# Scale maxima through memory, two jobs' score maxima beside the convolution, and gating and residual adds on GpSimd, in a two-layer hybrid backbone

## The chip, the cores and the metric

One core of one Trainium2 chip runs the whole kernel. TensorE multiplies, VectorE, ScalarE and GpSimd do elementwise work and reductions, and nearly every DMA is issued from SyncE's queue (SP). The metric is the device time of one execution in microseconds.

## The reference

A stream of 2048 latent tokens and 256 context tokens of width 1024 goes through two layers, in float32. What matters of it:

```
for layer in range(2):
    shift, scale, gate = split(silu(c) @ w_mod + b_mod)
    p = split_cols((rms_norm(h, norm_g) * (1 + scale) + shift) @ w_in)   # 1024 -> 3584 columns
    y_conv = p.cb * short_conv(p.cc * p.cv, conv_w) * silu(p.cz)         # width 3 over positions
    att    = softmax(q k^T / 8) v          # 4 heads of 64, 2 key heads; rms_norm and rotary on q, k
    hg     = rms_norm(forward + backward HGRN2 scan)                     # chunks of 64
    y_four = real part of the 2-D DFT over positions and channels
    y = concat(y_conv, att * silu(az), hg * silu(hz), y_four * silu(fz)) @ w_out
    h = h + gate * y                       # the context stream likewise, except in layer 1
out = rms_norm(h, final_g)
```

## The kernel before

Every matrix of float32 numbers is split into two float16 halves (high and low) after scaling by a power of two, and a product is three products of halves: high by high, low by high, high by low. The power of two comes from the largest absolute value of the matrix.

**A scale maximum.** `wsplit` (L385) takes a block of 256 columns of w_in: `absmax` (L153) gives the largest value in each of 128 partitions (VectorE), L391 joins the two halves, `rowmax` (L137) transposes the column of 128 into one row on TensorE and reduces it on VectorE (L142), `spread` (L145) multiplies that number by a row of ones on TensorE, so that every partition has it, and copies it out (L150). `pow2` makes the scale; ScalarE casts the high half (L406), VectorE makes the low half (L407). The same is done for the attention's values (`att_values`, L900), for w_out (`out_wmax`, L1557), and in `out_open` (L1587), where six bounds are transposed at once and give the scale of the output projection's input.

**A layer's stages.** `layer` (L1376) runs, one after another: the HGRN2 projections and forward scan; the reverse scan with gates and Fourier projections (`hg_reverse`); the Fourier transform; the attention projection (`att_block`, with gates, the maxima of w_out and four blocks of weights); then the convolution's projections (`conv_block`), the attention's four jobs of 512 queries, and the output projection (`out_tile`, 18 tiles of 128 tokens, 16 in layer 1).

A job has two parts. `att_max` (L931) computes scores of 128 queries by 512 keys on TensorE (L941) into two banks tagged "tr" and reduces each to its row maximum on VectorE (L942), 80 of them; the maxima are transposed and sent by DMA into two rows of Q2 (L960). `att_core` (L966) computes scores again with those rows in the product (L1016, L1017), takes the exponential on ScalarE (L1019), casts its high half on ScalarE (L1025) or VectorE (L1023), makes the low half on VectorE (L1026) and multiplies by the values (L983, L984), 72 steps for a job.

`weave` calls generators in turns, spread over a common course; an entry is (number of steps, generator, from, to). So the stages before the change are:

```
weave(values, maxima of job 0, a third of the convolution)
weave(core(jobs[0]), mx(jobs[1]), the rest of the convolution)
weave(core(jobs[1]), mx(jobs[2]), out_open, out tiles up to T[0] = 5)
weave(core(jobs[2]), mx(jobs[3]), out tiles up to T[1] = 8)
weave(core(jobs[3]), out tiles up to T[2] = 12)
```

and the remaining tiles go, in layer 0, beside the first weights and norms of layer 1 (`start`, L1396). The calls' order is a wish: the framework orders each engine's instructions by it and by its own estimate of when operands are there, so an engine may take a later call first. Within one engine, SP's queue too, instructions then start strictly in that order.

An output tile: `out_load` reads heads' outputs and gates, `out_prep` (L1259) multiplies them (L1266), splits the product and transposes both halves by DMA (L1271, L1272); 48 products of 512 columns follow (L1306), and VectorE multiplies by the gate vector (L1310) and adds the residual (L1311), half a tile each.

## Time and profile before

| | us |
|---|---|
| median of 3 runs | 2727.41 (2725.93 to 2731.69) |
| the profiled execution | 2724.91 |
| its span, first to last instruction | 2721.5 |
| TensorE busy | 2576.0 |
| VectorE busy | 2147.0 |
| ScalarE busy | 1495.4 |
| GpSimd busy | 105.0 |

The rows further below name engines PE (TensorE), DVE (VectorE), ACT (ScalarE), POOL (GpSimd) and SP. Matmuls overlap and their ends are modelled, so the spacing of their starts says more than their durations. An arrow points from what an instruction reads to what it writes, or from an idle time to what ended it.

### The profile page before, as it was taken

The numbers are of one execution on the slowest core, as the hardware profiler recorded it, in microseconds if no ns is written. First come the engines' busy times: TensorE is split into PE (matmuls) and PEld (weight loads), VectorE is DVE, ScalarE is ACT, GpSimd is POOL, SyncE is SP. The second block draws the span as 40 slices with busy tenths as digits, with TensorE's granted clock in tenths as the row PEclk, the third lists the DMA queues.
The fourth block names the chain that finished last, engine by engine and source line by source line (L and its number), as shares of the span: only waits on it lengthen the run. The fifth ranks groups of instructions, "written<-read, shape, count | busy, mean of one in ns | idle before, by whom it ended". The sixth has DMA issues, their size and how long they took to land. (4 is left out here: it accounts for less than half of the span.)

```text
span 2721.5 us, 67137 instructions
## 1 busy us (share of the span) xinstructions
PE 2576.0 (95%) x28046; PEld 1915.2 (70%) x28046; DVE 2147.0 (79%) x4707; ACT 1495.4 (55%) x2789; POOL 105.0 (4%) x108
## 2 busy tenths in 40 slices
PE   6999999999999999999999999999988999999998
PEld 3788877888777875555547888878877787455553
DVE  5888765777698669899877888768678876999885
ACT  2877532322226647798837666423221565879782
POOL 0000001011000000000000000010110000000000
PEclk8999999999999999999999999999999999999999
DMA  6111158353411015224281111344333100423425
GB/s 218 56 49 49 37 187 266 116 152 103 113 38 56 16 45 170 77 72 130 55 247 56 48 49 33 101 131 148 110 92 95 40 25 22 145 79 77 115 52 156
DMA packets 268680, 260.32 MB, mean 96 GB/s; under 512 B 95316, under 2 KB 237656, under 8 KB 268376
## 3 DMA queue, kind: packets, MB, share of 16 engines
q1 hardware_dynamic: 268376, 256.04, 31.5%
q8 instruction: 219, 3.59, 0.5%
q14 instruction: 85, 0.70, 0.1%
HBM read 168.59 MB, written 67.13 MB: 87 GB/s over the span
## 5 line engine op out<-in xcount | busy, mean ns | idle before, releaser
L431 PE MATMUL psmm<-xh,wh 128*128 128x256 f16 x2208 | 608.1, 275 | 7.8 <-DVE xh L357 6.1
L432 PE MATMUL psmm<-xl,wh 128*128 128x256 f16 x2208 | 606.7, 275 | 1.5 <-DVE xl L358 1.5
L433 PE MATMUL psmm<-xh,wl 128*128 128x256 f16 x2208 | 606.5, 275 | 0.7 <-DVE wl L407 0.7
L1019 ACT ACTIVATE aP<-pssc,pshift,ascale 128x512 f32<-128x512 f32 (+1 forms) x584 | 444.6, 778 | 221.6 <-PE pssc L1017 193.2
L445 PE MATMUL psmm<-wh,xh 128*128 128x256 f16 x1664 | 459.1, 276 | 5.6 <-ACT av L818 4.2
L1026 DVE TENSOR_TENSOR apl<-aP,aph 128x512 f16<-128x512 f32 (+1 forms) x584 | 390.2, 681 | 86.8 <-ACT aph L1025 82.6
L446 PE MATMUL psmm<-wl,xh 128*128 128x256 f16 x1664 | 458.4, 275 | 0.0
L447 PE MATMUL psmm<-wh,xl 128*128 128x256 f16 x1664 | 458.2, 275 | 0.0
L942 DVE TENSOR_REDUCE amx<-pstr 128x1 f32<-128x512 f32 (+1 forms) x648 | 391.5, 627 | 46.5 <-PE pstr L941 45.1
L1025 ACT CAST aph<-aP 128x512 f16<-128x512 f32 (+1 forms) x508 | 305.5, 619 | 9.6
L983 PE MATMUL pspv<-V,aph 128*128 128x129 f16 x2320 | 298.7, 221 | 1.4 <-DVE aph L1023 1.2
L984 PE MATMUL pspv<-V,apl 128*128 128x65 f16 x2320 | 269.6, 193 | 4.9 <-DVE apl L1026 3.6
L984 PEld LDWEIGHTS <-apl 128*128 128x128 f16 x2320 | 206.6, 98 | 84.4 <-DVE apl L1026 39.7
L983 PEld LDWEIGHTS <-aph 128*128 128x128 f16 x2320 | 214.6, 97 | 68.5 <-ACT aph L1025 9.4
L431 PEld LDWEIGHTS <-wh 128*128 128x128 f16 x2208 | 217.9, 99 | 59.4 <-issue 7.0
L432 PEld LDWEIGHTS <-wh 128*128 128x128 f16 x2208 | 217.8, 99 | 57.0 <-issue 5.8
L941 PE MATMUL pstr<-K,Q 128*128 128x512 f16 (+1 forms) x648 | 230.0, 362 | 13.3 <-DVE amx L942 8.8
L433 PEld LDWEIGHTS <-wl 128*128 128x128 f16 x2208 | 217.5, 99 | 34.2 <-issue 2.1
L1016 PE MATMUL pssc<-Q,K 128*128 128x512 f16 (+1 forms) x584 | 221.4, 379 | 4.2 <-ACT aP L1019 2.9
L1017 PE MATMUL pssc<-Q,K 66*128 66x512 f16 (+1 forms) x584 | 221.7, 382 | 0.0
L1306 PE MATMUL psmm<-xh,oyh 128*128 128x512 f16 x544 | 206.8, 380 | 1.9 <-DMA oyh<-oa 1.8
L1306 PE MATMUL psmm<-xl,oyh 128*128 128x512 f16 x544 | 206.7, 380 | 0.0
(310 smaller groups left out, 4228.5 us busy)
## 6 DMA issues: line engine op xcount, KB each, us to landing
wst<-w_in SPq DMA_DIRECT2D x56, 512.0 KB
wmod<-w_mod SPq DMA_DIRECT2D x18, 1024.0 KB
d_G<-nh SPq DMA_DIRECT2D x51, 256.0 KB
oo<-d_O SPq DMA_DIRECT2D x34, 384.0 KB
og<-d_G SPq DMA_DIRECT2D x34, 384.0 KB
d_h<-oh SPq DMA_DIRECT2D x18, 512.0 KB
nh<-d_h SPq DMA_DIRECT2D x18, 512.0 KB
nh<-x SPq DMA_DIRECT2D x16, 512.0 KB
```

The source lines that it names most:

```text
L431: nc.tensor.matmul(out, lhsT=wh[:, k, cs], rhs=a, start=(k == 0), stop=False)
L432: nc.tensor.matmul(out, lhsT=wh[:, k, cs], rhs=b, start=False, stop=False)
L433: nc.tensor.matmul(out, lhsT=wl[:, k, cs], rhs=a, start=False, stop=(k == KC - 1))
L445: nc.tensor.matmul(out, lhsT=a, rhs=wh[:, k, :], start=(k == 0), stop=False)
L446: nc.tensor.matmul(out, lhsT=a, rhs=wl[:, k, :], start=False, stop=False)
L447: nc.tensor.matmul(out, lhsT=b, rhs=wh[:, k, :], start=False, stop=(k == KC - 1))
L942: nc.vector.tensor_reduce(out=mx[:, h, j, i : i + 1], in_=ps[:, :w], axis=AX.X, op=ALU.max)
L983: nc.tensor.matmul(pv(j), lhsT=ph[:, t], rhs=self.V[:, s, kv, :], start=st, stop=False, skip_group_check=True)
L984: nc.tensor.matmul(pv(j)[:, 0:65], lhsT=pl[:, t], rhs=self.V[:, s, kv, 0:65], start=False, stop=sp and j % 2 == 1, skip_group_check=True)
L1019: nc.scalar.activation(out=P[:, :n], in_=ps[:, :n], func=AF.Exp, scale=self.ascale, bias=self.pshift)
L1026: nc.vector.tensor_sub(out=pl[:, :n], in0=P[:, :n], in1=ph[:, :n])
L1306: nc.tensor.matmul(ps, lhsT=y, rhs=w, start=(i == 0), stop=(i == len(mms) - 1))
```

## The change

- A scale maximum (`wsplit`, `out_wmax`, the values, `out_open`) no longer goes through TensorE. `far_put` stores the 128 partial maxima to memory, `far_get` loads all of them back into every partition, `far_max` reduces them there on VectorE. Four weight blocks (`quick`) keep the old way. The calls get one more step, and the weave's counts follow.
- The values' maximum is taken beside the last gates of the projection stage (`att_vmax`).
- `core(jobs[0])` and the convolution get the score maxima of jobs 1 and 2; `core(jobs[1])` gets those of job 3, `core(jobs[2])` none. Q1 and Q2 have three buffers.
- Output tiles are split at T = (5, 9, 13). `out_open` comes behind the last two weight rows and ahead of the first `out_load`, its steps are spread a little wider, and the tiles start later in the stage.
- The third job, like the fourth, casts three of eight high halves on VectorE.
- The product with the gates (L1266) and the residual add (L1311) go to GpSimd.
- Buffers: the gate vectors lie in a convolution input's place, `cth` shares `cc`'s three buffers, `rows` lies in a pool that closes.

```diff
@@ -134,6 +134,23 @@
+    def far_put(self, a):
+        d = self.dram.tile([128, a.shape[1]], F32, name=self.nm("far"))
+        self.nc.sync.dma_start(out=d, in_=a)
+        return d
+    def far_get(self, d, pool, tag="far", bufs=1):
+        n = d.shape[1]
+        w = self.t(pool, [128, 128 * n], F32, tag, bufs)
+        self.nc.sync.dma_start(out=w, in_=d.rearrange("p n -> (p n)").unsqueeze(0).to_broadcast([128, 128 * n]))
+        return w
+    def far_max(self, w, n=1):
+        r = self.t(self.small, [128, n], F32, f"farmax{n}")
+        self.nc.vector.tensor_reduce(out=r, in_=w.rearrange("p (q n) -> p n q", n=n), axis=AX.X, op=ALU.max)
+        return r
     def rowmax(self, a):
@@ -172,7 +189,7 @@
-    def setup(self):
+    def setup(self, pool):
         nc, ap, cst = self.nc, self.ap, self.cst
@@ -189,7 +206,7 @@
         self.masks = cst.tile([128, 6, 64], U16, name="masks")
-        rows = cst.tile([R_N, 128], F32, name="rows")
+        rows = self.t(pool, [R_N, 128], F32, "rows", 1)
@@ -366,11 +383,11 @@
-    def wprep(self, l, b, pool=None, pace=False):
+    def wprep(self, l, b, pool=None, pace=False, quick=False):
...
         yield
-        yield from self.wsplit(l, b, half, pool, pace)
+        yield from self.wsplit(l, b, half, pool, pace, quick)
@@ -382,7 +399,7 @@
-    def wsplit(self, l, b, half, pool=None, pace=False):
+    def wsplit(self, l, b, half, pool=None, pace=False, quick=False):
@@ -391,11 +408,16 @@
         yield
+        if quick:
+            m = self.rowmax(am)
+            yield
+        else:
+            d = self.far_put(am)
+            yield
+            w = self.far_get(d, self.small)
+            yield
         with slow():
-            m = self.rowmax(am)
-        yield
-        with slow():
-            sw, isw = self.pow2(self.spread(m), self.small, tag="sw")
+            sw, isw = self.pow2(self.spread(m) if quick else self.far_max(w), self.small, tag="sw")
             nc.vector.tensor_copy(out=ds[:, 3:4], in_=isw)
@@ -897,15 +919,21 @@
+    def att_vmax(self):
+        am = self.t(self.small, [128, 1], F32, "vam", 1)
+        self.nc.vector.tensor_reduce(out=am, in_=self.vmax, axis=AX.X, op=ALU.max)
+        d = self.far_put(am)
+        yield
+        w = self.far_get(d, self.atp, "av", 2)
+        yield
+        self.vscale, self.visc = self.pow2(self.far_max(w), self.cst, tag="avs")
+        yield
     def att_values(self, keep, pool):
         nc = self.nc
-        am = self.t(self.small, [128, 1], F32, "vam", 1)
-        nc.vector.tensor_reduce(out=am, in_=self.vmax, axis=AX.X, op=ALU.max)
-        m = self.rowmax(am)
-        yield
-        s, self.visc = self.pow2(self.spread(m), keep, tag="avs")
-        yield
+        s = self.vscale
         for a in range(0, NTT, 4):
@@ -920,8 +948,8 @@
         c = slice(job["tq"] * 128, job["tq"] * 128 + n)
-        Q1 = self.t(pool, [128, 4, 512], F16, "Q1", 2)
-        Q2 = self.t(pool, [66, 4, 512], F16, "Q2", 2)
+        Q1 = self.t(pool, [128, 4, 512], F16, "Q1", 3)
+        Q2 = self.t(pool, [66, 4, 512], F16, "Q2", 3)
         for r in range(2):
@@ -1068,7 +1096,7 @@
         nc.scalar.activation(out=z, in_=pz, func=AF.Copy, scale=wz[2][:, 2:3])
-        th = self.t(pool, [128, 512], F32, "cth", 1)
+        th = self.t(pool, [128, 512], F32, "cc", 3)
         nc.scalar.activation(out=th, in_=z, func=AF.Tanh)
@@ -1263,7 +1291,7 @@
         yl = self.t(pool, [128, KC, 128], F16, "oyl", 2)
-        nc.vector.tensor_mul(out=o, in0=o, in1=g)
+        nc.gpsimd.tensor_tensor(out=o, in0=o, in1=g, op=ALU.mult)
         a = self.t(pool, [128, 768], F16, "oa", 2)
@@ -1308,7 +1336,7 @@
             nc.vector.tensor_mul(out=t, in0=ps, in1=gb[:, c])
-            nc.vector.tensor_add(out=h[:, c], in0=h[:, c], in1=t)
+            nc.gpsimd.tensor_tensor(out=h[:, c], in0=h[:, c], in1=t, op=ALU.add)
             if half == 0:
@@ -1352,7 +1380,7 @@
         w = [self.mod_load(0, *todo[0], pool, 3)]
-        self.setup()
+        self.setup(pool)
         fr = [self.norm_front(0, 0, nm)]
@@ -1360,7 +1388,7 @@
             if i == 2:
-                run(self.wsplit(0, 7, half))
+                run(self.wsplit(0, 7, half, quick=True))
             run(self.mod_cols(0, x, w[i], mod, pool, "mm"))
@@ -1403,7 +1431,7 @@
-            weave(tail, (22, start(), 0.2, 0.9))
+            weave(tail, (26, start(), 0.2, 0.9))
@@ -1414,7 +1442,7 @@
             if l == 0:
-                w = [self.wprep(l, b) for b in (8, 9, 10)]
+                w = [self.wprep(l, b, quick=True) for b in (8, 9, 10)]
                 with self.after(last):
@@ -1445,7 +1473,7 @@
             for sb in range(1, NS):
-                weave((33, self.hg_proj(l, sb, hp)), (22, self.hg_levels(l, sb - 1, hp)), (8, norms(sb), 0.3, 1.0), *([(5, self.wprep(l, 13), 0.4, 0.8)] if sb == NS - 1 else []))
+                weave((33, self.hg_proj(l, sb, hp)), (22, self.hg_levels(l, sb - 1, hp)), (8, norms(sb), 0.3, 1.0), *([(6, self.wprep(l, 13), 0.4, 0.8)] if sb == NS - 1 else []))
             weave((22, self.hg_levels(l, NS - 1, hp)), chain(*gates(13, 512, some[:2])))
@@ -1460,7 +1488,7 @@
-        preps = lambda bs, pool=None: chain(*[(5, self.wprep(l, b, pool, b < 4)) for b in bs])
+        preps = lambda bs, pool=None: chain(*[(6, self.wprep(l, b, pool, b < 4)) for b in bs])
         fs = ExitStack()
@@ -1472,7 +1500,7 @@
                 chain(*gates(13, 512, some[2:]), *[(9, self.fourier_block(sb, 12)) for sb in some]),
-                (15, preps((12, 6, 4))[1], 0.1, 1.0),
+                (18, preps((12, 6, 4))[1], 0.1, 1.0),
             ]
@@ -1488,12 +1516,18 @@
             self.att_open(l, ab)
+            vm = self.att_vmax()
+            def one(g):
+                next(g)
+                yield
             weave(
...
                     merge(gates(6, 0, some[6:]) + gates(11, 256, some[:-3]), [(17, self.att_block(l, sb)) for sb in range(NS)]),
-                    late(), *gates(11, 256, some[-3:]),
+                    late(), *[x for sb in some[-3:] for x in (*gates(11, 256, [sb]), (1, one(vm)))],
                 ),
-                chain((10, self.out_wmax(l)), preps((1, 2, 3, 0), wc)),
+                chain((12, self.out_wmax(l)), preps((1, 2, 3, 0), wc)),
             )
@@ -1501,7 +1535,7 @@
         jobs = [dict(tq=2 + 4 * b, nq=4, nk=NTT) for b in range(4)]
-        jobs[-1]["dve"] = 3
+        jobs[-1]["dve"] = jobs[-2]["dve"] = 3
         jobs[-1]["last"] = True
@@ -1527,22 +1561,22 @@
             part = lambda sbs: chain(*[x for sb in sbs for x in conv[sb]])
-            weave((7, self.att_values(keep, at), 0.02, 0.2), (*chain(*pre, mx(jobs[0])), 0.25, 1.0), part(some[:n]), (*fetch(jobs[1]), 0.6, 0.7))
-            weave(core(jobs[0]), mx(jobs[1]), part(some[n:]))
+            weave((5, self.att_values(keep, at), 0.02, 0.2), (*chain(*pre, mx(jobs[0])), 0.25, 1.0), part(some[:n]), (*fetch(jobs[1]), 0.6, 0.7))
+            run(fetch(jobs[2])[1])
+            weave(core(jobs[0]), chain(mx(jobs[1]), mx(jobs[2])), part(some[n:]))
         wcs.close()
...
         t0 = 2 * s0
-        T = (5, 8, 12)
-        run(fetch(jobs[2])[1])
+        T = (5, 9, 13)
+        run(fetch(jobs[3])[1])
         weave(
             core(jobs[1]),
-            (*mx(jobs[2]), 0.05, 1.0),
-            (*chain((1, self.out_load(l, t0, ou)), *[(1, self.out_weights(k)) for k in (6, 7)], (3, self.out_open(l, ou))), *((0.0, 0.04) if need else (0.055, 0.08))),
-            (*out(range(t0, T[0])), 0.07 if need else 0.09, 1.0),
+            (*mx(jobs[3]), 0.05, 1.0),
+            (*chain(*[(1, self.out_weights(k)) for k in (6, 7)], (4, self.out_open(l, ou)), (1, self.out_load(l, t0, ou))), *((0.0, 0.08) if need else (0.02, 0.11))),
+            (*out(range(t0, T[0])), 0.12 if need else 0.14, 1.0),
         )
-        run(fetch(jobs[3])[1])
-        weave(core(jobs[2]), (*mx(jobs[3]), 0.05, 1.0), out(range(T[0], T[1])))
+        weave(core(jobs[2]), out(range(T[0], T[1])))
         weave(core(jobs[3]), out(range(T[1], T[2])))
@@ -1569,7 +1603,11 @@
         nc.vector.tensor_reduce(out=am, in_=mx, axis=AX.X, op=ALU.max)
-        self.ows, self.owi = self.pow2(self.allmax(am), self.cst, tag=f"ows{l}")
+        d = self.far_put(am)
+        yield
+        w = self.far_get(d, self.small)
+        yield
+        self.ows, self.owi = self.pow2(self.far_max(w), self.cst, tag=f"ows{l}")
         yield
@@ -1588,8 +1626,9 @@
         self.gbc = []
+        G = self.t(self.xp, [128, 2, D], F32, "xh2", 1)
         for s in range(2 if l < DEPTH - 1 else 1):
-            g = self.t(pool, [128, D], F32, f"gbc{s}", 1)
+            g = G[:, s]
             nc.sync.dma_start(out=g, in_=self.d_gate[l, s].unsqueeze(0).to_broadcast([128, D]))
@@ -1598,17 +1637,11 @@
         nc.vector.tensor_reduce(out=mx[:, 5:6], in_=self.vmax, axis=AX.X, op=ALU.max)
-        pt = self.bank("tr")
-        nc.tensor.transpose(pt[:6, :128], mx, self.id32)
-        m = self.t(self.small, [6, 1], F32, "om6", 1)
-        nc.vector.tensor_reduce(out=m, in_=pt[:6, :128], axis=AX.X, op=ALU.max)
-        dg = self.t(self.small, [6, 6], F32, "odg", 1)
-        nc.vector.tensor_scalar_mul(dg, self.id32[:6, :6], m)
-        yield
-        pt = self.bank("tr")
-        nc.tensor.matmul(pt[:, 0:6], lhsT=self.ones, rhs=dg, start=True, stop=True)
-        a = self.t(self.small, [128, 6], F32, "oam", 1)
-        nc.vector.tensor_copy(out=a, in_=pt[:, 0:6])
+        d = self.far_put(mx)
+        yield
+        w = self.far_get(d, pool, "oo", 2)
+        yield
+        a = self.far_max(w, 6)
         b = self.t(self.small, [128, 4], F32, "obd", 1)
...
         nc.vector.tensor_mul(out=b[:, 1:2], in0=self.hgm, in1=a[:, 1:2])
```

## Rows read from the trace of the kernel before

**Rows 1.** Busy time of each engine in stretches of the span, header first.

```profile
core 0: us, PE busy (x) PEld busy (x) DVE busy (x) ACT busy (x) POOL busy (x), PEclk, DMA share, GB/s
559.00:731.00 172.00, 157.66 (x1382) 137.52 (x1379) 120.50 (x258) 44.78 (x68) 21.77 (x9) 0.96 0.44 117
825.00:1008.00 183.00, 183.00 (x1801) 145.99 (x1799) 129.28 (x241) 113.97 (x169) 0.00 (x0) 1.00 0.07 21
1008.00:1023.00 15.00, 11.71 (x62) 4.72 (x61) 13.32 (x40) 2.81 (x4) 0.15 (x1) 0.67 0.77 239
1023.00:1148.00 125.00, 120.78 (x997) 67.45 (x995) 113.35 (x198) 99.28 (x150) 0.00 (x0) 1.00 0.37 111
1148.00:1260.00 112.00, 109.51 (x951) 61.63 (x947) 104.16 (x188) 97.10 (x155) 0.00 (x0) 1.00 0.29 80
1260.00:1361.00 101.00, 99.83 (x903) 56.13 (x903) 83.14 (x157) 82.01 (x126) 0.00 (x0) 1.00 0.37 104
1884.00:2051.00 167.00, 148.37 (x1299) 128.81 (x1296) 119.68 (x276) 42.68 (x67) 20.51 (x9) 0.97 0.43 122
2309.00:2325.00 16.00, 11.78 (x77) 5.40 (x75) 13.86 (x40) 3.64 (x6) 0.00 (x0) 0.79 0.85 262
2325.00:2429.00 104.00, 102.30 (x902) 57.70 (x900) 102.63 (x185) 96.65 (x156) 1.54 (x2) 1.00 0.29 83
2429.00:2544.00 115.00, 109.60 (x948) 61.08 (x948) 111.00 (x206) 100.26 (x169) 1.96 (x3) 1.00 0.28 78
2544.00:2648.00 104.00, 101.03 (x895) 55.06 (x893) 85.65 (x163) 85.15 (x140) 3.09 (x4) 1.00 0.37 101
```

**Rows 2.** Timeline of TensorE at two places: start, duration, line.

```profile
723.44 0.27 PE L140 MATMUL pstr<-id,vam 128*1 128x128 f32 x1
723.55 0.27 PE L431 MATMUL psmm<-xh,wh 128*128 128x256 f16 x1
...
1000.11 0.38 PE L1016 MATMUL pssc<-Q,K 128*128 128x512 f16 x1
1000.33 0.38 PE L1017 MATMUL pssc<-Q,K 66*128 66x512 f16 x1
```

**Rows 3.** TensorE's waits, 80:1008 and 1437:2310: us, times, longest.

```profile
PE pstr L148 <- DVE rowmax L142: 9.4, 3, 3.8
PE pstr L140 <- DVE wam L391: 2.0, 1, 2.0
...
PE pstr L140 <- DVE wam L391: 10.2, 3, 4.5
PE pstr L148 <- DVE rowmax L142: 9.6, 4, 2.7
```

**Rows 4.** The SP queue's waits, whole span: us, times, longest.

```profile
SPq L730 <- DMA d_O<-hQc: 24.5, 10, 4.1
...
SPq L1287 <- DMA d_h<-oh: 13.3, 6, 5.3
```

**Rows 5.** Timeline of SP and of ScalarE about 1009 to 1021 us.

```profile
1009.32 1.18 SPq L960 DMA_DIRECT2D Q<-amt  x2
...
1019.55 1.45 ACT L1019 ACTIVATE aP<-pssc,pshift,ascale 128x512 f32<-128x512 f32 x2 [8.53 <-PE pssc L1017]
```

**Rows 6.** Groups of VectorE's instructions, whole span: busy us, mean ns.

```profile
L942 DVE TENSOR_REDUCE amx<-pstr 128x1 f32<-128x512 f32 (+1 forms) x648 | 391.5, 627 | 46.5 <-PE pstr L941 45.1
L1026 DVE TENSOR_TENSOR apl<-aP,aph 128x512 f16<-128x512 f32 (+1 forms) x584 | 390.2, 681 | 86.8 <-ACT aph L1025 82.6
...
L1311 DVE TENSOR_TENSOR oh<-oh,ot 128x512 f32<-128x512 f32 x68 | 46.5, 684 | 0.4
...
L1266 DVE TENSOR_TENSOR oo<-oo,og 128x768 f32<-128x768 f32 x34 | 32.2, 952 | 8.8 <-DMA oo<-d_O 8.7
```

**Rows 7.** Groups of GpSimd's instructions, whole span: busy us, mean ns.

```profile
L171 POOL TENSOR_TENSOR arr<-arv,mhalf 128x12 f32<-128x12 f32 (+1 forms) x18 | 42.3, 2349 | 369.3 <-DVE arv L169 293.8 <-DVE p2e L123 75.5
...
L188 POOL MEMSET cact<- 128x256 f32 x1 | 0.3, 317 | 0.0
```

## The prediction

> **What bounds the kernel now.** I read the stretches of the span first, one per stage, because a share over the whole span mixes stages with different limits [rows 1]. In the attention projection (559 to 731 us, and 1884 to 2051 in the second layer) VectorE and ScalarE have air and TensorE is short of full by 14 and 19 us. The convolution with the first job's core (825 to 1008) is TensorE without a gap: 183.0 of 183 us, VectorE at 129. In the two stages after it VectorE carries 103 to 113 us of 104 to 125 us, and TensorE falls short where VectorE is fullest: the third job's stage takes 112 and 115 us although the last job's stage, which has one output tile more and no score maxima, takes 101 and 104. Between them lies a hole: from 1008 to 1023 TensorE runs at a mean clock of 0.67, ScalarE does 2.8 of 15 us, and 2309 to 2325 looks alike (0.79, 3.6 of 16).
>
> Then the price of TensorE's own work, from the spacing of its starts [rows 2]: 0.22 us for 512 columns, 0.11 us for the transpose of a maximum. So a full job of score maxima (64 products of 512 columns, 16 of 256) is 64 x 0.22 + 16 x 0.11 = 15.8 us, an output tile 48 x 0.22 = 10.6 us.
>
> Then its waits [rows 3]: it stands still 9.4 + 2.0 + 10.2 + 9.6 = 31.2 us for the two VectorE halves of a scale maximum (the maximum over rows, L391; over the transposed row, L142). That is TensorE waiting in the middle of its stream for an engine that is behind, for one number. The clock column of [rows 1] adds (1 - 0.96) x 172 + (1 - 0.97) x 167 = 12 us of lost speed in the two projection stages, where most of these waits lie.
>
> The kernel is thus bound by TensorE; what can be won is its holes.
>
> **Scale maxima through memory.** 28 of them lose their transposes and spreads: 24 weight blocks, two of the values, two of w_out; the two bounds of out_open go the same way. The four first blocks of layer 0 keep TensorE (quick). Removed: the 31.2 us of waits at most. I take two thirds, 21, since VectorE is as late as before, and ScalarE's weight cast, which waits for the scale, stands ahead of evictions of TensorE's two banks; 0 to 31.2 for the range. Of the 12 us of clock, half: 6 (0 to 12). Of TensorE's own instructions, a transpose and two spreads each, by the 0.11 us: 28 x 0.2 = 6 (3 to 9).
>
> Added: two transfers per maximum on SP's queue, where the load must wait for the store. Such a wait exists: d_op behind d_O, 24.5 us over 10, up to 4.1; and oh behind d_h, 13.3 over 6 [rows 4]. A round trip is then two landings of about 2.45 us plus two issues of 0.5, some 6 us, 9 at worst. Queued behind the waiting load on SP are w_in, d_G, nh and the transposes; behind the reduction on VectorE all its later work. Cover: the steps of the preparation are spread over their stage, in the projection 172 us over 36 steps, so store to use is 2 x 4.8 = 9.6 us, and more in the two stages before. It isn't covered in the tail of layer 0 (four blocks; some 2 us a step), in block 13 (two) and in out_open (two). For these eight I add 6 us: VectorE waits some 3 us, TensorE, with two full banks, a quarter of it (0 to 8 x 6 = 48).
>
> **Maxima of two jobs beside the convolution.** 15.8 us of products per layer go from the third job's stage to the convolution, where TensorE has no gap: +15.8. VectorE gets 80 reductions of 0.627 us [rows 6], 50: 129 + 50 = 179 of 199 us, 90%. That such a load is bearable is seen at 2325 to 2429: VectorE 102.6 of 104 us, TensorE 102.3. I add 3 us a layer for stalls (0 to 11, the third job's overhang over the fourth, 112 - 101 and 115 - 104).
>
> The third job's stage then holds what the fourth does now, four tiles and no maxima (its casts are split 3 of 8 too): 112 to 101 and 115 to 104, -11 each (0 to -14). The tail loses a tile, -10.6. So the work itself cancels (+15.8 + 10.6 - 15.8 - 10.6) and what stays is slack: -11 - 10.6 + 15.8 + 3 = -3 a layer, -6. Layer 0's tail also carries the next layer's first weights and norms, a chain that doesn't shrink: +5 (0 to 10).
>
> The hole at 1008 is a gain of its own. The second job's maxima end with the first job's core; their row goes to SP at 1009.3 and the first scores come to ScalarE at 1019.55, after 8.5 us of nothing [rows 5]. After the change that row is sent in mid convolution, and scores can follow at once. What stays: out_open's bound, now a round trip of 6 us instead of two transposes, and output tiles that start at 0.12 of the stage instead of 0.07, so that TensorE has only the core and the maxima for some 15 us. I take 6 us of each hole, 12 in all (0 to 20: ten of each).
>
> **GpSimd.** Per output tile VectorE gives away 0.952 + 2 x 0.684 = 2.3 us [rows 6], 34 tiles. Only in the second job's stage is it near its limit: -4 for both layers (8 tiles). GpSimd has no such instruction in the trace. Its rows are a fill of 256 elements in 0.317 us and a power of 12 in 2.35 [rows 7]: if two reads and a write each go at the fill's pace, some 1.2 ns, a product of 768 takes 2.8 us and an add of 512 1.9; VectorE's own 0.95 and 0.68 are the lower end, the power's 2.35 us for 12 elements no guide to so plain an operation. A tile lasts 10.6 us, so even 6.6 us of GpSimd is covered by the tile ahead, except at the end of the kernel, where one add stands in the last chain: +1.
>
> The Trainium skill speaks against this part ("SBUF — State Buffer", Who interferes with whom): a VectorE instruction with two inputs in SBUF and a GpSimd instruction that reads SBUF share a port pair, and the later one is blocked for all of the earlier. No row here shows GpSimd reading a large tile. By that rule the relief would be nothing or a loss; it is the third rival.
>
> The remaining edits (rows in another pool, cth in cc's three buffers, Q in three, the gate vectors in xh2, value scale computed ahead) I cost at nothing: each buffer's former reader lies one convolution block or a stage back.
>
> **Sum.** -21 - 6 - 6 + 6 - 6 + 5 - 12 - 4 + 1 = -43. The profiled execution took 2724.9 us (span 2721.5): 2682 us. The median of the runs shown is 2727.4, 2.5 above, so I forecast 2684.
>
> **Rivals.**
> First: the round trip takes the wait's place. VectorE and ScalarE wait for memory, evictions come late, TensorE stops for a full bank instead of a transpose. For it: ScalarE's evictions and casts share one queue. Against: 9.6 us of cover. The first three terms shrink to the 6 of TensorE's own work: +27, 2711. Chance 0.18.
> Second: VectorE becomes the bound of the convolution; the stage overhangs by 11 us a layer, not 3: +16, 2700, and with a piece of the hole back 2708. For it: the overhang is seen where VectorE is at 104 of 112. Against: 2325 to 2429. Chance 0.15.
> Third, the port: in the second job's stage a tile blocks VectorE for up to 6.6 us in place of the 2.3 it gave away, 4.3 x 8 tiles = 34 at worst; about half of VectorE's work there has two SBUF inputs (72 subtractions L1026 of 0.681 us, 49 of 103 us), so 17, with the 4 lost: 2705. Chance 0.1.
> Fourth, slower than before: SP's queue. Each of the 30 round trips holds SP for a landing; if weights, transposes and loads behind it come that much late and nothing covers it, 30 x 2.45 = 74, less the 6 counted: 2752. It decides from (2727 - 2684 + 6) / 30 = 1.6 us of TensorE's time per round trip. Against: SP's loads run a tile or a block ahead. Chance 0.09.
> Fifth: nothing measurable, when rivals one to three come together: 2722 to 2733, chance 0.06.
> Sixth: the holes close wholly, -31.2, -12, -20: 2684 - 10 - 6 - 8 = 2660 and, with no cost in tail and convolution (5 and 6), 2649. Chance 0.08.
>
> **Numbers.** The forecast, with 2668 to 2699 of its own, has 0.34. A measurement of this kernel can't tell less than 0.2%, 5.5 us, from no change. Faster: 0.34 + 0.18 + 0.15 + 0.1 + 0.08 = 0.85; same 0.06; slower 0.09. The range 2652 to 2724 leaves out the fourth, most of the fifth and a part of the sixth.
>
> **What would show it.** TensorE's waits for L142 and L391's successors nearly gone after 90 us, and the projection stages 8 to 14 us shorter each; a stage of the convolution some 19 us longer; no 8 us without scores at the second job's start; the third job's stage near 101 us with its maxima gone. I am wrong if TensorE's waits reappear under ScalarE's evictions or a far load, if the convolution's stage grows by 25 us or more, or if VectorE's two-input subtractions (L1026) become longer or start late behind GpSimd.

## The result and the profile after

The changed kernel takes **2906.4 us** (2904.2 to 2912.9 in 4 runs) against 2729.6 us (2725.9 to 2733.9) for the kernel before on the same chip: a ratio of 1.0651, 95% interval 1.0627 to 1.0676. It is 177 us slower; 2684 was forecast, with a range of 2652 to 2724. The profiled execution has a span of 2902.1 us and a mean granted clock of 0.953 (before: 2721.5 and 0.982).

First the busy time by stretch in the kernel after. The first row is the stage ahead of the attention projection, where blocks 12, 6, 4, 5 and 11 of the weights are prepared; then the projection, the convolution with the first job, the second and the third job, and the second layer's projection, second and third job; they answer to [rows 1].

```profile
core 0: us, PE busy (x) PEld busy (x) DVE busy (x) ACT busy (x) POOL busy (x), PEclk, DMA share, GB/s
349.00:594.00 245.00, 215.90 (x2581) 175.50 (x2579) 148.73 (x407) 77.21 (x165) 15.30 (x12) 0.94 0.58 168
594.00:767.00 173.00, 162.54 (x1439) 143.07 (x1438) 122.25 (x262) 44.56 (x67) 21.76 (x9) 0.97 0.44 113
868.00:1069.00 201.00, 199.38 (x1878) 153.60 (x1876) 172.23 (x320) 115.07 (x169) 0.00 (x0) 1.00 0.08 26
1069.00:1210.00 141.00, 131.59 (x1055) 71.47 (x1053) 123.40 (x219) 102.81 (x154) 25.01 (x17) 0.99 0.42 119
1210.00:1319.00 109.00, 101.92 (x927) 58.78 (x925) 84.35 (x137) 86.32 (x127) 20.10 (x13) 0.98 0.32 93
2003.00:2195.00 192.00, 160.56 (x1401) 140.28 (x1400) 120.12 (x266) 41.27 (x68) 20.50 (x9) 0.92 0.41 104
2480.00:2604.00 124.00, 115.49 (x966) 64.09 (x964) 119.12 (x218) 101.96 (x161) 17.00 (x12) 0.96 0.37 102
2604.00:2719.00 115.00, 103.61 (x926) 59.03 (x924) 89.64 (x148) 89.66 (x142) 22.86 (x17) 0.99 0.31 88
```

The convolution grew from 183 to 201 us, full as before: the moved maxima. The stages that prepare weights have gaps, and most of them grew: 245 us with 215.9 of TensorE (the same stage takes 221 with 212.8 in a kernel of the experiments that has the moves alone), and 192 with 160.6, 31 us short, where [rows 1] has 167 with 148.4, 19 short. The first layer's projection takes 173 us, about what it took before (172). In the stages with output tiles TensorE falls short by 7 to 11 us though VectorE has more air than before (84 of 109 us in the third job against 104 of 112).

Then the waits: engine, line, what was waited for; sum, times, longest, in us. L151 reduces a maximum that came back from memory, L146 loads it, L428 is the cast of a weight block, which needs its scale.

```profile
ACT wh L428 <- DVE sw L129: 265.3, 25, 22.4
DVE farmax L151 <- DMA far<-far: 174.5, 25, 16.7
SPq L146 <- DMA far<-wam: 140.8, 21, 8.9
SPq L146 <- DMA far<-vam: 31.0, 4, 8.9
PE psmm L467 <- ACT ax L849: 23.5, 3, 14.6
PE psmm L453 <- ACT cc L1081: 17.6, 1, 17.6
PE psmm L453 <- ACT fu L1136: 16.7, 2, 9.5
```

VectorE stands 174.5 us at the reduction and SP 172 us at the load. TensorE's waits for scale maxima [rows 3] have become waits for ScalarE's evictions. One round trip in the projection shows how they hang together, in four pieces of the timeline (SP, VectorE, ScalarE, TensorE: start, duration, line):

```profile
652.48 0.49 SPq L140 DMA_DIRECT2D far<-wam  x1
660.25 0.33 SPq L146 DMA_DIRECT2D far<-far  x1
660.62 2.49 SPq L900 DMA_TRANSPOSE akt<-aks  x2
...
665.15 0.29 DVE L151 TENSOR_REDUCE farmax<-far 128x1 f32<-128x128 f32 x1 [3.13 <-DMA far<-far]
...
666.30 2.19 ACT L428 ACTIVATE wh<-wst,sw 128x1024 f16<-128x1024 f32 x2 [10.09 <-DVE sw L129]
668.40 0.66 ACT L849 ACTIVATE ax<-psmm,ds 128x512 f32<-128x512 f32 x1
...
669.11 0.27 PE L467 MATMUL psmm<-wh,xh 128*128 128x256 f16 x1 [3.30 <-ACT ax L849]
```

The store is issued at 652.48; the load, which waits for its landing, only at 660.25, 7.8 us later. Behind it on SP the transposes wait. The loaded row is there at 665.15, after VectorE has stood 3.13 us; ScalarE, with the weight cast at the head of its queue, has stood 10.09 us for the scale, and the eviction behind that cast comes late, so that TensorE stops 3.30 us for its bank. From store to reduction: 12.7 us, where the prediction had 6, at worst 9; the median of the 30 round trips is 13.5 us.

GpSimd's new instructions, and VectorE's beside them: busy time and mean ns, then the idle time before. First the kernel after:

```profile
L1339 POOL TENSOR_TENSOR oh<-oh,ot 128x512 f32<-128x512 f32 x68 | 97.6, 1436 | 536.0 <-DVE ot L1338 501.4 <-DVE ams L977 12.2 <-DVE p2e L123 11.6
L1294 POOL TENSOR_TENSOR oo<-oo,og 128x768 f32<-128x768 f32 x34 | 65.1, 1927 | 434.4 <-DMA oh<-d_h 327.2 <-DMA oo<-d_O 58.9 <-DMA oyc<-d_yc 15.1
L1054 DVE TENSOR_TENSOR apl<-aP,aph 128x512 f16<-128x512 f32 (+1 forms) x584 | 423.8, 733 | 93.5 <-ACT aph L1053 85.5 <-PE pssc L1045 0.9
L1302 DVE SCALAR_TENSOR_TENSOR oyl<-oyc,osc,oyh 128x256 f16<-128x256 f32 x34 | 25.7, 756 | 0.0
```

The same two lines of VectorE in the kernel after without its GpSimd edits:

```profile
L1054 DVE TENSOR_TENSOR apl<-aP,aph 128x512 f16<-128x512 f32 (+1 forms) x584 | 394.2, 682 | 78.5 <-ACT aph L1053 72.9 <-DVE aph L1051 0.5
L1302 DVE SCALAR_TENSOR_TENSOR oyl<-oyc,osc,oyh 128x256 f16<-128x256 f32 x34 | 16.2, 477 | 0.0
```

The subtraction with two operands in SBUF (L1026 of before, 681 ns in [rows 6]) goes from 682 to 733 ns, the low half of the gate from 477 to 756. GpSimd itself is quicker than estimated: 1.44 us an add (1.9), 1.93 us a product (2.8).

### The profile page after: what moved, and what is told of

Read it like the earlier page. It is cut to its first block, busy times and chain, and to the rows that moved or that the text cites. A ratio compares the mean times of both kernels' runs of the same rounds, so it can differ in the third digit from the quotient of the medians.

```text
span 2902.1 us, 67164 instructions
## 1 busy us (share of the span) xinstructions
PE 2587.1 (89%) x27956; PEld 1922.5 (66%) x27956; DVE 2172.2 (75%) x4637; ACT 1477.7 (51%) x2725; POOL 268.3 (9%) x210
## 5 line engine op out<-in xcount | busy, mean ns | idle before, releaser
L1054 DVE TENSOR_TENSOR apl<-aP,aph 128x512 f16<-128x512 f32 (+1 forms) x584 | 423.8, 733 | 93.5 <-ACT aph L1053 85.5
L1011 PE MATMUL pspv<-V,aph 128*128 128x129 f16 x2320 | 291.9, 222 | 0.7 <-DVE aph L1051 0.6
L1012 PE MATMUL pspv<-V,apl 128*128 128x65 f16 x2320 | 269.4, 194 | 18.0 <-DVE apl L1054 17.4
L1053 ACT CAST aph<-aP 128x512 f16<-128x512 f32 (+1 forms) x444 | 268.9, 613 | 10.6
L969 PE MATMUL pstr<-K,Q 128*128 128x512 f16 (+1 forms) x648 | 229.2, 359 | 24.5 <-DVE amx L970 17.9
L1044 PE MATMUL pssc<-Q,K 128*128 128x512 f16 (+1 forms) x584 | 222.8, 382 | 30.2 <-ACT aP L1047 28.9
L1334 PE MATMUL psmm<-xh,oyh 128*128 128x512 f16 x544 | 213.8, 393 | 24.9 <-DMA oyh<-oa 9.9
L1334 PEld LDWEIGHTS <-oyh 128*128 128x128 f16 x1088 | 108.4, 100 | 161.2 <-issue 29.3
```

What stands on the lines that cost most here:

```text
L1011: nc.tensor.matmul(pv(j), lhsT=ph[:, t], rhs=self.V[:, s, kv, :], start=st, stop=False, skip_group_check=True)
L1012: nc.tensor.matmul(pv(j)[:, 0:65], lhsT=pl[:, t], rhs=self.V[:, s, kv, 0:65], start=False, stop=sp and j % 2 == 1, skip_group_check=True)
L1054: nc.vector.tensor_sub(out=pl[:, :n], in0=P[:, :n], in1=ph[:, :n])
L1334: nc.tensor.matmul(ps, lhsT=y, rhs=w, start=(i == 0), stop=(i == len(mms) - 1))
```

## The experiments

Theory A lays the loss on the round trips: the store lands late, and SP, VectorE and ScalarE stand in line for it. Theory B lays it on GpSimd. The runs were made in several groups on three chips, each group with its own runs of the kernel before (medians 2725 to 2730), so parts are compared by ratio: a hundredth is 27.3 us.

**The change in parts.** Four kernels: the change with all these maxima back on TensorE; the change with product and add back on VectorE; both undone, so that only the moves are left; and the kernel before with the GpSimd edits alone.

```diff
 # maxima back on TensorE (all four places)
-            d = self.far_put(am)
-            yield
-            w = self.far_get(d, self.small)
+            m = self.rowmax(am)
 # back on VectorE
-        nc.gpsimd.tensor_tensor(out=o, in0=o, in1=g, op=ALU.mult)
+        nc.vector.tensor_mul(out=o, in0=o, in1=g)
-            nc.gpsimd.tensor_tensor(out=h[:, c], in0=h[:, c], in1=t, op=ALU.add)
+            nc.vector.tensor_add(out=h[:, c], in0=h[:, c], in1=t)
```

> The changed kernel with every scale maximum back on TensorE (transposes and spreads as before); moved score maxima, GpSimd and tiles kept. Theory A (the round trip through memory is what costs: in the changed kernel VectorE stands 174 us before the loaded maxima, and the stages without output tiles are 110 us longer): about 2906 - 110 - 20 in the tails = 2776 us. Theory B (GpSimd holding VectorE's port is what costs): little changes, above 2860. Theory C (the moved maxima overload the convolution and its neighbours): above 2860 too.

Measured: 2762.4 us, 1.0136 (1.0112 to 1.0160).

> The changed kernel with the product with the gates and the residual add back on VectorE, the rest kept. Theory A: the stages of the third and fourth job lose some 7 to 10 us each, tails and second job some more, together 30 to 45: about 2868 us. Theory B: near or below 2740. VectorE's subtraction L1054 should go back from 733 to 681 ns under both, if the port is what lengthened it.

Measured: 2841.6 us, 1.0420 (1.0398 to 1.0441).

> Scale maxima on TensorE and no elementwise work on GpSimd: of the change only the moved score maxima, the tiles' split, the third job's casts and the buffers are left. Theory A and B: what the prediction gave for this part, 2705 to 2725 us (the hole at the second job's start closed, the third job near 101 us). Theory C: above 2760.

Measured: 2704.0 us, 0.9922 (0.9899 to 0.9946).

> The kernel before with the two GpSimd edits alone. If GpSimd's reads hold up VectorE's instructions with two inputs in SBUF: 30 to 60 us slower than before (2760 to 2790), with L1026 some 50 ns longer, most in the stages with output tiles. If it only takes work from VectorE, as the prediction had it: 0 to 5 us faster.

Measured: 2773.9 us, 1.0177 (1.0158 to 1.0197).

The moves alone gain 21 us. On top of them GpSimd costs (1.0136 - 0.9922) x 2727 = 58 us, and 48 alone; the round trips cost (1.0420 - 0.9922) x 2727 = 136. Together -21 + 58 + 136 = 173 of the 178 that the ratio of the whole change gives: both theories hold a part, A the larger. Theory A's times for the first two kernels, 2776 and 2868, were 14 and 26 us too high; the fourth lies in the range for reads that hold up VectorE. In the moves alone the stretches are as forecast (convolution, second, third job; the third of layer 1):

```profile
830.00:1030.00 200.00, 198.74 (x1869) 152.88 (x1868) 172.15 (x322) 114.23 (x168) 0.00 (x0) 1.00 0.08 26
1030.00:1167.00 137.00, 131.94 (x1070) 73.15 (x1069) 125.85 (x237) 103.60 (x157) 0.15 (x1) 0.99 0.44 120
1167.00:1270.00 103.00, 100.04 (x913) 58.28 (x911) 78.72 (x148) 85.28 (x125) 0.00 (x0) 0.98 0.37 98
2436.00:2539.00 103.00, 100.52 (x924) 58.28 (x922) 86.22 (x168) 89.37 (x142) 3.05 (x4) 1.00 0.35 98
```

**GpSimd: the port or the chain.** VectorE keeps all its work, and GpSimd multiplies and adds a constant vector into a tile that nobody reads.

```diff
         nc.vector.tensor_mul(out=o, in0=o, in1=g)
+        du = self.t(pool, [128, 768], F32, "dum", 1)
+        nc.gpsimd.tensor_tensor(out=du, in0=self.gbc[0][:, 0:768], in1=self.gbc[0][:, 0:768], op=ALU.mult)
```

(and so beside each add, with 512 columns.)

> The kernel before, with all its work left on VectorE, and beside each output tile's gate product and residual adds a GpSimd product of 768 and adds of 512 on the constant gate vector, into a tile that nobody reads. Theory, the memory port: GpSimd's mere reading costs VectorE its two-input instructions, so the time is near that of the kernel in which GpSimd does the work (ratio 1.0177 to before), 2755 to 2800. Rival, the chain: GpSimd's slower add and product only lengthen the way from bank to h and from o to its transposes; then work aside costs nothing, 2722 to 2738.

Measured: 2798.8 us, 1.0265 (1.0232 to 1.0298): 72 us slower, though no output tile waits for these results. Its subtraction on VectorE, and GpSimd's adds:

```profile
L1026 DVE TENSOR_TENSOR apl<-aP,aph 128x512 f16<-128x512 f32 (+1 forms) x584 | 425.6, 742 | 86.3 <-ACT aph L1025 82.4
L1315 POOL TENSOR_TENSOR dum<-gbc 128x512 f32<-128x512 f32 x68 | 90.4, 1329 | 5.9 <-DVE gbc L1628 0.7
```

584 subtractions at 742 instead of 681 ns are 35 us by themselves. But the work didn't stay beside the output tiles: it needs nothing of them, and GpSimd ran all of it back to back in two stretches, 1033 to 1119 us and 2375 to 2447 us of the span. VectorE's busy time and number of subtractions (L1026) in the first stretch and behind it, then the granted clock:

```profile
1033.00:1119.00 86.00, 38.73 (x30) 0.88 0.41 118
1119.00:1360.00 241.00, 104.08 (x154) 1.00 0.31 87
```

That is 1.29 us each beside GpSimd and 0.68 us without (1.30 and 0.67 in the second layer). VectorE's reduction of scores in a bank (L942), one operand and none in SBUF, takes 0.62 us in both, ScalarE's exponential (L1019) 0.77 and 0.75. So GpSimd's work in SBUF holds up VectorE's two-operand work there, without any chain. Here the trace agrees with the rule that the prediction weighed against this part, the Trainium skill's "SBUF — State Buffer" (Who interferes with whom).

The 72 us are no price for the same work spread over the tiles. The stretches fall into the second job's stages, where VectorE is nearly full [rows 1], and when the second ends, VectorE has stood 12.4 us for a power of the final norm that lay behind this work in GpSimd's queue. So what VectorE's relief is worth can't be read from them.

Nor do they rule out the chain in the change itself. In the kernel after, GpSimd makes a gate product as soon as its heads' outputs are loaded; ScalarE's high half of it (L1297) stands in ScalarE's queue ahead of an exponential, and TensorE waits for that:

```profile
1234.98 3.56 POOL L1294 TENSOR_TENSOR oo<-oo,og 128x768 f32<-128x768 f32 x2 [6.38 <-DMA oo<-d_O]
1236.81 0.94 ACT L1297 ACTIVATE oa<-oo,osc 128x768 f16<-128x768 f32 x1 [2.34 <-POOL oo L1294]
...
1238.98 0.38 PE L1044 MATMUL pssc<-Q,K 128*128 128x512 f16 x1 [3.34 <-ACT aP L1047]
```

Over the span ScalarE waits 61.2 and 52.8 us for GpSimd's products and sums; without the GpSimd edits it waits 33.0 and 25.2 us for VectorE's. TensorE waits 28.9 us for exponentials, 6.3 without the edits. How the 48 to 58 us divide between the port and the chain stays open.

A second kernel leaves only the add on GpSimd, on the moves alone.

```diff
-            nc.vector.tensor_add(out=h[:, c], in0=h[:, c], in1=t)
+            nc.gpsimd.tensor_tensor(out=h[:, c], in0=h[:, c], in1=t, op=ALU.add)
```

> The moves alone (2704.0) with only the residual add on GpSimd. In the kernel after 68 adds of 1.44 us take 97.6 us of GpSimd and 34 products of 1.93 us 65.1 us. Theory, the port: the loss goes with the time for which GpSimd reads, 60% of the 58 us, so 2730 to 2745. Rival, the product carries it (it stands at the head of the chain to the transposed gate rows): 2700 to 2715. Other rival, the add carries it all, as it stands between the output tile and h: 2755 to 2765.

Measured: 2746.7 us, 1.0056 (1.0036 to 1.0077), by the ratio (1.0056 - 0.9922) x 2727 = 37 us or 63% of the 58, as the time of reading has it (60%); the median is 2 us above the stated range. Neither the product nor the add carries it all; a chain that grows with the same durations would give this share too.

**The round trips: who pays.** Scales come from TensorE as in the moves alone, and each of the 24 weight blocks also makes its round trip, whose result nobody uses; in a second kernel VectorE also reduces the loaded row where the kernel after does.

```diff
+            m = self.rowmax(am)
             d = self.far_put(am)
             yield
             w = self.far_get(d, self.small)
             yield
         with slow():
+            self.far_max(w)          # second kernel only
-            sw, isw = self.pow2(self.far_max(w), self.small, tag="sw")
+            sw, isw = self.pow2(self.spread(m), self.small, tag="sw")
```

> The moves alone (2704.0) with the scales from TensorE's transposes, and beside each weight block the same store and load on SP as in the kernel after; nobody reads what is loaded. SP's queue thus waits as in the kernel after, VectorE and ScalarE don't. Theory, the wait for the loaded maximum on VectorE, and for its scale on ScalarE, is what costs: 2700 to 2735. Rival, SP's queue costs (transposes and loads stand behind the waiting load): 2790 to 2845.

Measured: 2775.9 us, 1.0181 (1.0165 to 1.0198).

> As the run before it, and VectorE reduces the loaded row at the place where the kernel after does, ahead of the scale's own instructions; the scale still comes from TensorE's transposes and the reduced value is not used. Theory, VectorE's wait costs: most of the way to the 2841.6 of the kernel after without GpSimd, 2790 to 2850. Rival, SP's queue costs: the same as the run before it, within 15 us.

Measured: 2834.9 us, 1.0414 (1.0387 to 1.0441).

Neither range of the first held: SP's waiting alone costs 71 us (1.0181 - 0.9922), VectorE's 64 more (1.0414 - 1.0181), which brings the time to that of the real scheme (1.0420, with six round trips more). Both rivals have half. SP's part arrives as late transfers: in the first kernel TensorE waits 12.3, 9.3 and 6.7 us for the Fourier table, Q and the modulation weights, none of them among its waits in the moves alone. ScalarE's wait for the scale is no third part: 238.5 us in the real scheme without the GpSimd edits, 110.3 in the last kernel, though both take the same time. In that last kernel TensorE still makes all its transposes and waits 32.6 us for the two halves of a maximum, 2.2 in the real scheme; to take that away, as the change does, gained nothing that can be seen beside this.

**The store.** Is a store of 128 single numbers slow in itself? A first probe put stores of five widths into the kernel before:

> The kernel before with ten extra pairs of transfers on SP in the first layer's convolution stage: a store of 128 rows from the identity to memory, then a load of one row of it that has to wait for the store. Widths: a is 1 number a row, packed; b is 1 number a row, each 64 bytes apart in memory; c is 6, d 16, e 128 numbers a row, packed; the five follow one another twice. The time of the kernel is not the point, the time from store to load is. Theory, the narrow store is slow in itself: a takes 7 to 16 us until the load can start, as in the kernel after (typically 8 to 9), c 3.6 to 4.6 us, d and e under 4 us; b tells whether it is the 4 bytes (then b is like a) or neighbours within one piece of memory (then b is like c). Rival, the queue was merely full in the kernel after: all five widths take the same, within 1.5 us.

```diff
+        nc.sync.dma_start(out=d[:, 0:w], in_=self.id32[:, 0:w])
+        yield
+        nc.sync.dma_start(out=back[:, 0:w], in_=d[0:1, 0:w])
```

Measured: 2729.9 us in one run, and no answer: no data tied the stores to a place; they were issued from 53 us of the span on among others, and their loads came in queue order. The second probe chains each round trip to the one before:

```diff
+        nc.sync.dma_start(out=d[:, 0:w], in_=src[:, 0:w])
+        nc.sync.dma_start(out=back[:, 0:w], in_=d[0:1, 0:w])
+        yield
+        nc.vector.tensor_copy(out=src[0:1, 0:1], in_=back[:, 0:1])
```

> The kernel before with eight extra round trips on SP in the first layer's convolution stage, each chained to the one before by a VectorE copy of what was loaded, so that none can start early: a store of 128 rows, then a load of one row of it, which waits for the store. a is 1 number a row, packed; b 1 number a row, 64 bytes apart in memory; c 6, d 16 numbers a row, packed; the four follow one another twice. Theory, a store of one number a row is slow in itself: a holds the load for 7 to 9 us as in the kernel after, c and d for 3.6 to 4.6; b like a if the 4 bytes are the cause, like c if it is neighbours in one piece of memory. Rival, the load on the queue made it slow: in this quiet stage (the DMA engines are busy for less than a tenth) all four hold it equally, 2.5 to 4 us.

Measured: 2730.5 us in one run. Its timeline of SP, second passage (prba: 4 bytes a row, packed; prbb: 4 bytes, 64 apart; prbc: 24 bytes; prbd: 64 bytes):

```profile
791.90 0.32 SPq L168 DMA_DIRECT2D prba<-psrc  x1
799.12 0.24 SPq L169 DMA_DIRECT2D pback<-prba  x1
...
826.97 0.33 SPq L174 DMA_DIRECT2D prbb<-psrc  x1
830.38 0.25 SPq L175 DMA_DIRECT2D pback<-prbb  x1
832.88 0.33 SPq L180 DMA_DIRECT2D prbc<-psrc  x1
835.19 0.24 SPq L181 DMA_DIRECT2D pback<-prbc  x1
837.58 0.32 SPq L186 DMA_DIRECT2D prbd<-psrc  x1
839.02 0.24 SPq L187 DMA_DIRECT2D pback<-prbd  x1
```

From store to load: 7.2 us packed, 3.4 us with the rows 64 bytes apart, 2.3 and 1.4 us for wider rows. The first passage has 7.9, 6.7, 1.5 and 4.4 us; there SP issued other transfers between store and load of the first two pairs, so these two are bounds from above, and the 3.4 us rest on one pair. The 7.2 us fall in a stretch in which SP issues nothing else, so a full queue isn't the cause. Widening the stores of the round trips aside is the test of what this costs: each row holds sixteen copies, and the load reads as many bytes as before.

```diff
-            d = self.far_put(am)
+            am16 = self.t(self.small, [128, 16], F32, "am16", 2)
+            nc.vector.tensor_copy(out=am16, in_=am.to_broadcast([128, 16]))
+            d = self.far_put(am16)
```

> As the round trips aside (2775.9, scales from TensorE, nobody reads what is loaded), but each store carries sixteen copies of the maximum a row instead of one, and the load, of the same size as before, reads the first eight rows of it. Theory, the slow landing of the narrow store is what SP's queue pays with: the wait between store and load falls from 7 to 9 us to 2 to 4, and the time goes more than half of the way back to the moves alone, 2705 to 2740. Rival, any waiting pair costs it, or the transfers themselves: 2760 to 2785.

Measured: 2717.0 us, 0.9955 (0.9941 to 0.9970): of SP's 71 us, 9 are left. SP's waits for the store, with narrow and then with wide rows (two kernels):

```profile
SPq L146 <- DMA far<-wam: 142.8, 23, 12.1
```

```profile
SPq L148 <- DMA far<-am: 29.9, 17, 5.4
```

**Distance and queue.** Three kernels, all on the change without its GpSimd edits (2841.6), try to live with the slow store: the reduction four steps later; the transfers issued by GpSimd instead of SP; three steps more between store and load and three more before the reduction.

```diff
 # later reduction (left), both ends apart (right)
             w = self.far_get(d, ...)      d = self.far_put(am)
             yield                         yield
+            yield                     +   yield          (x3)
+            yield                         w = self.far_get(d, ...)
+            yield                         yield
+            yield                     +   yield          (x3)
 # transfers by GpSimd
-        self.nc.sync.dma_start(out=d, in_=a)
+        self.nc.gpsimd.dma_start(out=d, in_=a)      (and the load)
```

> The kernel after with gate product and residual add back on VectorE (as in the run that took 2841.6), and the reduction of a weight block's loaded maxima placed four steps of its preparation later, behind the load. Theory, VectorE stands in line: the round trip of 13 to 14 us is long, but nothing needs it at once; the loss comes from VectorE waiting at a reduction that stands too early in its order. Then four steps more (some 10 to 15 us) take most of the 157 us of these waits away, and the time falls to 2730 to 2780. Rival, SP stands in line: the load waits on SP for the store and holds transposes and loads behind it; the reduction's place changes little, 2815 to 2850.

Measured: 2813.0 us, 1.0307 (1.0275 to 1.0339).

> The kernel after with gate product and residual add back on VectorE (as in the run that took 2841.6), and the store and the load of each scale maximum issued by GpSimd instead of SP, which leaves SP's queue free of these waits. Theory, VectorE stands in line: its 157 us of waits for the loaded maxima stay, and so does the time, 2815 to 2860. Rival, SP stands in line: transposes and loads behind the waiting load come on time again, 2720 to 2780.

Measured: 2884.1 us, 1.0568 (1.0538 to 1.0599).

> The kernel after with gate product and residual add back on VectorE (2841.6), three more steps between a weight block's store and its load, and three more between the load and the reduction. Theory, all is a matter of distance: SP and VectorE find the transfers landed, and the time comes near the moves alone, 2700 to 2740. Rival, the round trip only moves into the chain of a weight block (its staging buffers are held longer, the next block's load comes later, the casts end later): 2780 to 2840.

Measured: 2804.7 us, 1.0275 (1.0234 to 1.0315).

The third lies in its rival's range and the first 2 us under its own rival's; the first gives back 31, the third 40 of 136 us. A block's steps share one stretch, so that more of them make each shorter: VectorE's wait goes from 157.2 to 119.7 and 108.7 us. And SP reaches the load early whatever stands between: in the third it waits 121.6 us for the stores of the weight blocks, 138.3 without the distance. The second is above both of its ranges: SP is free, but GpSimd's queue now holds the waits, for the maximum as well as for the store, and behind them stand its powers for the norms (VectorE's wait for them at L873 goes from 32.8 to 70.7 us):

```profile
DVE farmax L151 <- DMA far<-far: 177.9, 18, 14.5
POOL far L146 <- DMA far<-wam: 173.6, 21, 10.5
POOL far L140 <- DVE wam L408: 121.7, 16, 13.3
```

**The whole scheme with a quick store.** VectorE transposes the maximum in blocks of 32, and the same 128 numbers are stored as four rows of 128 bytes; load, reduction and scale as in the change, still without GpSimd's arithmetic.

```diff
+        self.nc.vector.tensor_copy(out=u, in_=a.to_broadcast([128, 32]))
+        self.nc.vector.transpose(out=v, in_=u)
-        self.nc.sync.dma_start(out=d, in_=a)
+        self.nc.sync.dma_start(out=d.rearrange("(q p) n -> q (p n)", q=4), in_=v[0:128:32])
```

> The kernel after with gate product and residual add back on VectorE (2841.6), where VectorE transposes each maximum in blocks of 32, so that the store writes four rows of 128 bytes instead of 128 rows of 4; load, reduction and scale as before. Theory, the narrow store is the root of both shares: store to load falls to 2 to 4 us, VectorE's wait for the loaded row to less than half of 157 us, and the time to 2720 to 2770. Rival, VectorE's share stays, since the load alone takes 3 to 6 us to land: 2770 to 2800.

Measured: 2721.3 us, 0.9981 (0.9967 to 0.9994). A store and its load on SP, and then the waits for the loaded row and for the store:

```profile
642.84 0.55 SPq L147 DMA_DIRECT2D far<-far  x1
...
644.93 0.34 SPq L153 DMA_DIRECT2D far<-far  x1
```

```profile
DVE farmax L158 <- DMA far<-far: 53.4, 15, 11.0
SPq L153 <- DMA far<-far: 24.4, 20, 4.5
```

Store to load takes 2.1 us here, 2.3 us in the median of 28 pairs. (1.0420 - 0.9981) x 2727 = 120 of the 136 us are gone, with a change to nothing but the shape of the store and two VectorE instructions that make it; VectorE's wait falls from 157.2 to 53.4 us. For the rival, that the load alone keeps VectorE waiting, at most the remaining 16 us are left.

> As the run before it, with three more steps between store and load and three more between load and reduction (the spaced run with narrow stores took 2804.7). Theory: 2700 to 2740, near the moves alone (2704.0) and not under the moves with spaced transposes (2696.6). Rival, the distance pushes the casts out as in the spaced run, so that it is no better than the run before it: 2740 to 2780.

Measured: 2714.6 us, 0.9957 (0.9942 to 0.9972). With a quick store distance helps by 7 us; memory still isn't better than TensorE's transposes (0.9922).

**A better version.** The moves alone, with one more step before a maximum's transpose and one before its spread:

```diff
+        yield
         with slow():
             m = self.rowmax(am)
         yield
+        yield
```

> The moves alone (2704.0), with one more step between a weight block's maximum and its transpose, and one more between the transpose's maximum and the spread: TensorE reaches each later, nothing goes by memory. Theory, what TensorE loses to scale maxima (16.1 and 6.5 us of waits in that kernel) is a matter of distance, and so is the 100 us that ScalarE waits for a scale: 2685 to 2700. Rival, the distance only moves the weight casts later, into the next projection's start: 2700 to 2730.

Measured: 2696.6 us, 0.9894 (0.9880 to 0.9909): the fastest of all, 29 us under before. Its TensorE waits 7.8 us for the maximum and 4.8 for its row; in the moves alone that is 16.1 and 6.5. The two intervals overlap, so the last 8 us over the moves alone are likely rather than sure.

## Why the prediction was wrong, step by step

**The step that failed: "A round trip is then two landings of about 2.45 us plus two issues of 0.5, some 6 us, 9 at worst".** Store to load alone took 7.3 to 12.7 us in the kernel after, and once 15.7 (28 stores of one number a row). The 2.45 us isn't a landing: it is 24.5 us over 10 waits [rows 4], what SP still had to stand when the load's turn came, and it belongs to other transfers, of 256 KB. The store of 128 rows of 4 bytes had no row in the trace of before, and its bound from above should have been far higher. With it fell the "9.6 us of cover": 12.7 us in the example above don't fit. The sum had 6 us for eight trips without cover and nothing for SP's standing. The terms for scale maxima, -21 - 6 - 6 + 6 = -27, measured +136: 71 by SP's standing in line, 64 by VectorE's, and next to nothing back from TensorE's saved waits. The gain failed by itself too: TensorE's waits for L391 and L142 did go (2.4 us are left of 34.0 over the whole span), but even with the quick store the part costs 16 us where -27 was forecast. Where it went was named: "I am wrong if TensorE's waits reappear under ScalarE's evictions or a far load".

**The clock.** -6 was forecast. By the prediction's own formula the second layer's projection, at 0.92 where [rows 1] has 0.97, loses (0.08 x 192) - (0.03 x 167) = 10 us instead, an estimate, beside TensorE's new gaps; the first layer's, at 0.97 against 0.96, gains 2.

**The moves: right.** The convolution grew by 17 us in the moves alone and 18 in the change (200 and 201 against 183; forecast 15.8 + 3), the third job takes 103 us in both layers (101 and 104). The terms -6 + 5 - 12 = -13 measured -21. By stage the profile of the moves alone has +17 and +17 us for the convolution, -9 and -12 for the third job, -3 and -5 for the second job with its hole (137 for 15 + 125, 115 for 16 + 104), where 6 each were taken, and -10 and -8 for the tails: -13 in all, and a span 14 us shorter, in the slowest of its four executions. The hole at the second job's start closed: ahead of its first scores ScalarE stands 1.59 us in the kernel after, where [rows 5] has 8.53:

```profile
1067.55 0.78 ACT L1047 ACTIVATE aP<-pssc,pshift,ascale 128x512 f32<-128x512 f32 x1 [1.87 <-PE pssc L1045]
...
1070.56 2.36 ACT L1047 ACTIVATE aP<-pssc,pshift,ascale 128x512 f32<-128x512 f32 x3 [1.59 <-PE pssc L1045]
```

The sign "the third job's stage near 101 us" holds without GpSimd (103 in both layers); in the kernel after it takes 109 and 115.

**GpSimd: wrong sign.** -4 + 1 was forecast, +48 to +58 measured. The mechanism stood as the third rival, but bounded to one stage ("4.3 x 8 tiles = 34 at worst") and halved; the runs show a loss in every stage with output tiles, since even where VectorE's busy time has air its instructions stand between ScalarE and TensorE in the core's chain: TensorE waits 17.4 us for the subtraction in the kernel after, 8.5 without GpSimd. That the longer way through GpSimd is "covered by the tile ahead" failed as well: TensorE's wait for ScalarE's exponentials grew by 22.6 us. How the loss divides between the two is open.

**The rivals.** The fourth had the right side: SP's queue "30 x 2.45 = 74", beside a measured 71. That agreement is half luck: 24 trips held SP 142.8 us, more than twice as long as assumed, and half of it reached the end. What it lacked was VectorE's half and GpSimd's. The first ("the round trip takes the wait's place") describes the path well and stopped at the loss of the gain, +27, because it took the six microseconds for granted.

What stays open: why packed rows of 4 bytes land later than the same rows 64 bytes apart. The Trainium skill ("DMA: Bandwidth & Descriptors", Specifications) says that transfers under 512 bytes are read, modified and written. The trace doesn't show that: 24, 64 and 128 bytes are below that figure too and were quick. That packed rows wait for each other because they share a piece of memory is a guess, which 7.2 against 3.4 us would fit.

## What to carry to other kernels

Before a value goes through memory, price the very store: its row length in bytes and how rows are packed, not the landing of another transfer; 128 single numbers, packed, were the worst shape tried, and a transpose in blocks of 32 mended it. A wait at the head of an in-order queue is paid for on each queue that holds it: here SP's cost 71 us and VectorE's 64. Work given to GpSimd isn't free of VectorE when both read SBUF. A dummy operation beside the unchanged kernel shows that in one run, but prices it only if it depends on the same data as the real work; otherwise it runs in another place, and denser.

## What the runs showed of the hardware

A store of 128 rows of 4 bytes, packed, held its reader 7.2 us in a stretch in which its queue was otherwise empty; the same numbers as four rows of 128 bytes 2.1 us (median of 28 pairs 2.3). GpSimd took 1.44 us for an add of 128x512 and 1.93 us for a product of 128x768, and VectorE's two-operand instructions beside it grew by 7% on the mean of a whole kernel (682 to 733 ns) and by 59% (477 to 756 ns) for the gate's low half, which belongs to the output tile itself. Beside GpSimd work without a pause the subtraction took 1.29 us instead of 0.68, and the reduction of scores in a bank took its 0.62 us. A cast on VectorE from one SBUF operand was held too: 2.04 us at 1224.89 us of the kernel after, beside GpSimd's products, and 0.42 us on the mean without them.
